# A prompt and sample step of a hybrid decoder: the sample's state updates in four row tiles, C against both halves of the states in one bank

## Chip, cores and metric

One core of a Trainium2 chip runs the whole step. The metric is the device time of one execution in microseconds; lower is better. The kernel before was timed in three runs.

## What is computed

One layer of a decoder trunk on a prompt of 16 + 256 tokens and on 8 samples of 4 tokens each: a SwiGLU block, a token mixer and a second SwiGLU block, each behind an RMSNorm. The mixer has a gated short convolution and a state-space branch. All matrices are float32; the kernel multiplies in a split of each operand into a high and a low part. The part that matters here is the state-space branch for the samples, in which the carried state of each sample (32 heads x 64 x 128) is read by C and brought up to date:

```python
xdt = x * dtc[..., None]
decay = jnp.exp(acs[:, :, -1:] - acs)
states = jnp.einsum('bcsgn,bcsgr,bcsgrp->bcgrpn', bc, decay, xdt)
chunk_decay = jnp.exp(acs[:, :, -1])
def step(h, inp):
    s, d = inp
    return h * d[..., None, None] + s, h
y_off = jnp.einsum('bcqgn,bcgrpn,bcqgr->bcqgrp', cc, h_prev, jnp.exp(acs))
```

For a sample, `states` sums over 4 tokens only, and there is one chunk. The new state of all 8 samples is an output of 8 MB, as is the old one an input.

## The kernel before

**The main stream.** `program` lists all products with weights as tiles of 128 x 128, in order: ffn1, the input projection (ga, dt, x, ac, ah, ab), ya, z, gb, yb, wo, ffn2. `drive` (L231) walks that list. Each tile is three matmuls (L255 to L257): high weight by high input, high by low, low by high, into a PSUM bank of the pool `psm` (4 banks, tag "m"). Weights come by DMA on SP, 8 tiles at a time, and are split three such units ahead: ACT copies the high part (L183), DVE subtracts (L184).

**The side work.** Two generators do the state-space scan beside the main stream: `Scan.prompt` for the prompt and `Scan.sample` for the samples, and before them `Scan.setup`. `drive` counts up `wanted["due"]` by a rate per main tile and calls `side_step` for each whole one: it takes the generators in turn and lets one run to its next `yield`. From ac to z (384 main tiles) the rate is RATE2. What is left when gb comes is emitted by `flush_side`. The side's PSUM banks are those of the pool `pss` (4 banks, tag "s").

**Order.** The code's order is not yet the order on an engine: the tile framework schedules each engine's instructions by priority in program order and by a simulated readiness, so that a side matmul that is not ready lets main matmuls pass. On the chip each engine then runs its list in order.

**The sample's part.** The 8 samples are two halves q of four samples j. For each group g of 8 heads the 4 states of a half lie in `ht`, [128 state rows, 4 samples, 512], loaded by `load` and stored by `store` on SP (L1051, L1104), with three buffers.
- `tokens(g)` (L1068) turns the group's x into rows of tokens by four transposes (L1078), multiplies by dt (L1082) and by the decay (L1060), and splits it into `xst`; then the same for the prompt's last 16 tokens into `xl`.
- For each half (L1113 on): `bm` is B masked for each of the four samples (L1125). C times the four states (L1131) goes to four strips of 32 columns of one bank. ACT copies it (L1133), four transposes (L1138) turn it, and DVE multiplies it into `yo` (L1141).
- For each sample: DVE decays the state (L1150), one matmul of `bm[:, j]` and `xst` over all 128 rows makes the update (L1152), DVE adds it (L1153). Each update has a bank of its own.
- At the end of a group DVE finishes the sample's y and calls `ready`; once the z tiles, two prompt `outputs` and the sample of a group are through, its norm is made, and after gb `scaled_splits` (L299, L300, L293) makes the operands of yb.

**The prompt's part.** For each half group `hg`: `tokens`, `weights`, `states` (L983 to L991), `outputs` (L1003 to L1021), each of one or a few steps.

**The set-up.** `setup` makes dt, the cumulated decays and the rows of B in the x stage, with small matmuls over 16, 32 or 128 rows (L781 to L807).

## Time and profile before

| | us |
|---|---|
| median of three runs | 881.52 (880.02 to 881.68) |
| the profiled execution | 881.86 |
| its span, from the first to the last instruction | 880.0 |
| PE busy | 868.8 (99%) |
| DVE busy | 621.3 (71%) |
| ACT busy | 496.2 (56%) |

The span is what the profile sees of one execution; the time has a little before and after it. Busy time is time in which an engine has at least one instruction under way. Matmuls overlap each other in a row of them, so that the sum of their durations is more than the time they take; the distance between two starts is what one costs. The scan runs beside the stages ac to z, from about 350 to 557 us; gb follows to 583 us, then yb.

### The profile page before, as it was taken

How to read it: one execution, taken by the hardware profiler on the slowest of the kernel's cores; microseconds unless marked ns; L12 is line 12 of the kernel's file. 1: busy time of each engine (PE TensorE's matmuls, PEld its weight loads, DVE VectorE, ACT ScalarE, POOL GpSimd, SP SyncE). 2: the span in 40 equal slices, each digit the busy share in tenths (PEclk: the TensorE clock that was granted, in tenths of full speed). 3: DMA queues.
4: the chain of work that ended last, by engine and by line, in shares of the span. 5: the costliest groups of instructions: out<-in, count | busy, mean ns of one | idle time of the engine just before them, and what ended most of it. 6: DMA issues, size and time to landing. Idle time of an engine off the chain costs nothing.

```text
span 880.0 us, 16239 instructions
## 1 busy us (share of the span) xinstructions
PE 868.8 (99%) x6448; PEld 849.8 (97%) x6448; DVE 621.3 (71%) x996; ACT 496.2 (56%) x899; POOL 53.4 (6%) x86
## 2 busy tenths in 40 slices
PE   9999999999999999999999999999999999999996
PEld 7999999999999999999999899999999999999996
DVE  6756666554677798799988999886676666665443
ACT  8543434343667787966655687774465444444442
POOL 0000000000012233001000211100000000000000
PEclk9999999999999999999999999999999999999999
DMA  8554545454644545865666655755555555555541
GB/s 299 190 155 157 165 147 167 146 166 150 201 166 146 153 153 171 314 211 202 231 223 225 242 198 174 257 183 169 167 168 166 164 165 166 163 164 168 169 139 54
DMA packets 45851, 158.69 MB, mean 180 GB/s; under 512 B 7168, under 2 KB 9504, under 8 KB 43472
## 3 DMA queue, kind: packets, MB, share of 16 engines
q1 hardware_dynamic: 45344, 157.21, 54.6%
q8 instruction: 50, 0.82, 0.4%
q10 hardware_dynamic: 432, 0.46, 0.2%
q14 instruction: 25, 0.20, 0.1%
HBM read 145.34 MB, written 12.31 MB: 179 GB/s over the span
## 4 chain that ended last, share of the span: by engine, by line
PE 97%; DVE 1%; ACT 1%; DMA 1%; SPq 0%; issue 0%; DVEq 0%
PE ps_d L257 6%; PE ps_d L256 5%; PE ps_d L255 5%; PE ps_u L257 5%; PE ps_g L255 5%; PE ps_u L256 5%; PE ps_u L255 5%; PE ps_g L257 5%; PE ps_g L256 5%; PE ps_x L255 3%; PE ps_x L256 3%; PE ps_x L257 3%; PE ps_z L255 2%; PE ps_z L257 2%; PE ps_yb L257 2%; PE ps_yb L255 2%
## 5 line engine op out<-in xcount | busy, mean ns | idle before, releaser
L184 DVE TENSOR_TENSOR wlo<-wraw,whi 128x1024 fp32r<-128x1024 f32 (+2 forms) x250 | 300.6, 1204 | 188.8 <-ACT whi L183 188.1
L183 ACT ACTIVATE whi<-wraw 128x1024 fp32r<-128x1024 f32 (+2 forms) x250 | 259.6, 1041 | 296.8 <-issue 182.8
L257 PE MATMUL ps_d<-hh,wlo 128*128 128x304 f32 (+1 forms) x352 | 105.6, 300 | 0.0
L255 PE MATMUL ps_d<-hh,whi 128*128 128x304 f32 (+1 forms) x352 | 105.0, 299 | 0.0
L256 PE MATMUL ps_d<-hl,whi 128*128 128x304 f32 (+1 forms) x352 | 104.7, 298 | 0.0
L256 PEld LDWEIGHTS ps_d<-hl,whi 128*128 128x128 f32 x352 | 66.7, 189 | 0.0
L257 PEld LDWEIGHTS ps_d<-hh,wlo 128*128 128x128 f32 x352 | 66.2, 188 | 0.0
L255 PEld LDWEIGHTS ps_d<-hh,whi 128*128 128x128 f32 x352 | 66.1, 188 | 0.0
L255 PE MATMUL ps_x<-unh,whi 128*128 128x304 f32 x192 | 58.8, 309 | 0.7 <-ACT dtraw L735 0.7
L256 PE MATMUL ps_x<-unl,whi 128*128 128x304 f32 x192 | 58.8, 307 | 0.0
L257 PE MATMUL ps_x<-unh,wlo 128*128 128x304 f32 x192 | 58.6, 306 | 0.0
L255 PE MATMUL ps_g<-n1h,whi 128*128 128x304 f32 x176 | 54.1, 308 | 0.7 <-ACT whi L183 0.7
L256 PE MATMUL ps_u<-n1l,whi 128*128 128x304 f32 x176 | 53.6, 304 | 0.0
L255 PE MATMUL ps_u<-n1h,whi 128*128 128x304 f32 x176 | 53.5, 304 | 0.0
L256 PE MATMUL ps_g<-n1l,whi 128*128 128x304 f32 x176 | 53.4, 304 | 0.0
L257 PE MATMUL ps_g<-n1h,wlo 128*128 128x304 f32 x176 | 53.1, 303 | 0.0
L257 PE MATMUL ps_u<-n1h,wlo 128*128 128x304 f32 x176 | 52.9, 302 | 0.0
L257 PE MATMUL ps_g<-n2h,wlo 128*128 128x288 f32 x176 | 52.3, 297 | 0.0
L255 PE MATMUL ps_u<-n2h,whi 128*128 128x288 f32 x176 | 52.2, 297 | 0.0
L257 PE MATMUL ps_u<-n2h,wlo 128*128 128x288 f32 x176 | 52.1, 296 | 0.0
L255 PE MATMUL ps_g<-n2h,whi 128*128 128x288 f32 x176 | 51.9, 295 | 0.0
L256 PE MATMUL ps_u<-n2l,whi 128*128 128x288 f32 x176 | 51.4, 292 | 0.0
(342 smaller groups left out, 2435.6 us busy)
## 6 DMA issues: line engine op xcount, KB each, us to landing
wraw<-wst SPq DMA_DIRECT2D x241, 512.0 KB, 3.5
h<-h SPq DMA_DIRECT2D x8, 1024.0 KB, 5.0
o_hs<-h SPq DMA_DIRECT2D x8, 1024.0 KB, 4.3
acb<-cumd SPq DMA_DIRECT2D x8, 512.0 KB, 4.3
wraw<-wst SPq DMA_DIRECT2D x7, 256.0 KB, 6.4
hd<-h SPq DMA_DIRECT2D x1, 1216.0 KB, 6.6
h<-hd SPq DMA_DIRECT2D x1, 1216.0 KB, 8.3
o_hp<-hf SPq DMA_DIRECT2D x8, 128.0 KB, 2.8
```

The lines of the kernel that those rows point to most:

```text
L183: act.activation(hi[:, a:b], r[:, a:b], AF.Copy)
L184: dve.tensor_tensor(out=lo[:, a:b], in0=r[:, a:b], in1=hi[:, a:b].bitcast(F32), op=ALU.subtract)
L255: te.matmul(o, lhsT=wh, rhs=xh, start=first, stop=False)
L256: te.matmul(o, lhsT=wh, rhs=xl, start=False, stop=False)
L257: te.matmul(o, lhsT=wl, rhs=xh, start=False, stop=last)
```

## The change

- C times the states is done once for each group: both halves accumulate in one bank, the second half's rows beside the first's, by a C operand that is zero elsewhere (`cc`). There are four evictions by ACT and 16 transposes of its result.
- The rows of tokens are laid out anew (`rows`, `sample_rows`): each strip of 32 rows has the tokens of two samples, one of each half, four times over (the parts of the split). `bm` masks by half only, so there are two masks per group. The update of sample j uses rows 32j to 32j + 31 alone.
- The four updates of a half go out as one group, j from 3 to 0, in four banks: three of `pss` and one of `psm`. Each is kept in program order behind the matmul traced before it, and the next main matmul behind them (`pin`).
- All decays of a half are done before. The step before the updates sets `hold`, and the prompt's generator idles at its yields until the updates are out.
- The prompt's last 16 tokens share one layout with the samples' 32 rows (`mixed`, `mixed_rows`); the small matmuls of the set-up use 48 rows, and column masks `kd` are added up there.
- `store` is called one step before the updates of the next half. RATE2 goes from 0.33 to 0.36.

```diff
-RATE2 = 0.33
+RATE2 = 0.36
...
-                te.matmul(o, lhsT=wh, rhs=xh, start=first, stop=False)
+                ins = te.matmul(o, lhsT=wh, rhs=xh, start=first, stop=False)
+                if clock.pop("pin", False):
+                    tc.keep_in_program_order(ins)
...
+    ssd.pin = lambda: clock.update(pin=True)
...
+        self.mixed(reps[:, 0:1], raw.unsqueeze(1))
+        self.rows(xp, reps[:, 1:2], raw[:, S0:T].unsqueeze(1))
...
-        dl = da[0:NL, 2]
+        dx = da[0:NX, 2]
         te.matmul(pv[:, 0], lhsT=K[:, C_GT:C_GT + P], rhs=da[:, 0], start=True, stop=True)
         te.matmul(pv[:, 1], lhsT=K[:, C_GT:C_GT + P], rhs=da[:, 1], start=True, stop=False)
-        te.matmul(pv[:, 1], lhsT=K[0:NL, C_ONE:C_ONE + P], rhs=dl, start=False, stop=True)
-        te.matmul(pv[:, 2], lhsT=gtl.rearrange("p k t -> p (k t)"), rhs=dl, start=True, stop=True)
-        te.matmul(pv[:, 3], lhsT=K[0:32, C_GTS:C_GTS + P], rhs=da[0:32, 3], start=True, stop=True)
+        te.matmul(pv[:, 1], lhsT=one, rhs=dx, start=False, stop=True)
+        te.matmul(pv[:, 2], lhsT=gtl, rhs=dx, start=True, stop=True)
+        te.matmul(pv[:, 3], lhsT=gtr, rhs=dx, start=True, stop=True)
         te.matmul(pv[:, 4], lhsT=K[:, C_ONE:C_ONE + P], rhs=da[:, 1], start=True, stop=False)
-        te.matmul(pv[:, 4], lhsT=K[0:NL, C_ONE:C_ONE + P], rhs=dl, start=False, stop=True)
+        te.matmul(pv[:, 4], lhsT=one, rhs=dx, start=False, stop=True)
...
+        kd = self.kd = self.t("kd", [P, 6])
+        for i, bs in enumerate(((4, 5, 6, 7), (2, 3, 6, 7), (0, 2, 4, 6), (1, 3, 5, 7))):
+            dve.tensor_tensor(out=kd[:, i:i + 1], in0=K[:, C_BM + bs[0]:C_BM + bs[0] + 1],
+                              in1=K[:, C_BM + bs[1]:C_BM + bs[1] + 1], op=ALU.add)
+            for b in bs[2:]:
+                dve.tensor_tensor(out=kd[:, i:i + 1], in0=kd[:, i:i + 1], in1=K[:, C_BM + b:C_BM + b + 1], op=ALU.add)
+        dve.tensor_scalar(out=kd[:, 4:6], in0=kd[:, 0:2], scalar1=2.0, scalar2=-1.0, op0=ALU.mult, op1=ALU.add)
+        dve.tensor_tensor(out=kd[:, 5:6], in0=kd[:, 4:5], in1=kd[:, 5:6], op=ALU.mult)
+
...
+    def mixed(self, out, x):
+        act, n = self.nc.scalar, out.shape[1]
+        k = P // NL - 2
+        act.activation(out[:, :, 0:NB * NT], x[:, :, S0:T], AF.Copy)
+        for j in range(n):
+            act.activation(out[:, j, NB * NT:].rearrange("p (k t) -> p k t", t=NL),
+                           x[:, j, TL:S0].unsqueeze(1).to_broadcast([P, k, NL]), AF.Copy)
+    def rows(self, pl, out, x):
+        act, (p, n, _) = self.nc.scalar, out.shape
         self.n += 1
-        r = pl.tile([P, 4, P // n, n], F32, name=f"four{self.n}", tag="tmp", bufs=2)
-        src = self.xs[:, c0:c0 + 4, a:a + n].unsqueeze(2).to_broadcast([P, 4, P // n, n])
-        for j in range(4):
-            self.nc.scalar.activation(r[:, j], src[:, j], AF.Copy)
-        return r.rearrange("p j k t -> p j (k t)")
+        t = pl.tile([p, n, 4, 2, NT], F32, name=f"rows{self.n}", tag="rows", bufs=1)
+        for q in range(2):
+            act.activation(t[:, :, :, q], x[:, :, 16 * q:16 * q + 16].rearrange("p n (i t) -> p n i t", t=NT), AF.Copy)
+        for j in range(n):
+            act.activation(out[:, j].rearrange("p (i c w) -> p i c w", c=4, w=2 * NT),
+                           t[:, j].rearrange("p i q t -> p i (q t)").unsqueeze(2).to_broadcast([p, 4, 4, 2 * NT]),
+                           AF.Copy)
+    def sample_rows(self, pl, c0):
+        self.n += 1
+        r = pl.tile([P, 4, P], F32, name=f"srows{self.n}", tag="tmp", bufs=2)
+        self.rows(pl, r, self.xs[:, c0:c0 + 4, S0:T])
+        return r
...
+        for _ in steps():
+            yield
+            while self.hold:
+                yield
...
-        def splits(name, pv, dtr, bufs):
-            xr = self.t("xrs", [P, 8, HD], bufs=2, tag="tmp")
-            dve.tensor_tensor(out=xr, in0=pv, op=ALU.mult, in1=dtr.unsqueeze(2).to_broadcast([P, 8, HD]))
-            xf = xr.rearrange("p h d -> p (h d)")
-            o = self.t(name, [P, 512], bufs=bufs, dt=F32R)
-            act.activation(o, xf, AF.Copy)
-            dve.tensor_tensor(out=o[64:P], in0=xf[64:P], in1=o[64:P].bitcast(F32), op=ALU.subtract)
-            return o
         def tokens(g):
             hs = slice(8 * g, 8 * g + 8)
-            xt[g] = self.t("xdts", [NX, 8, HD])
-            for o, i in ((xst, 3), (self.xl, 2)):
-                if i == 2:
-                    rep[g] = self.four(self.sp, 4 * g, True)
-                    yield
+            def turned(src):
                 p = self.ps()
-                src = rep.pop(g)
                 for j in range(4):
                     te.transpose(p[:, j * P:(j + 1) * P], src[:, j], ident)
-                del src
-                pv = p.rearrange("p (h d) -> p h d", h=8)
-                a = slice(0, NS) if i == 3 else slice(NS, NX)
-                dve.tensor_tensor(out=xt[g][a], in0=pv[a], op=ALU.mult,
-                                  in1=self.dt[a, i, hs].unsqueeze(2).to_broadcast([a.stop - a.start, 8, HD]))
-                if i == 2:
-                    while self.xl:
-                        yield
-                o[g] = splits("xst" if i == 3 else "xl", pv, self.dtr[:, i, hs], i - 1)
+                return p.rearrange("p (h d) -> p h d", h=8)
+            def decayed(pv, i, a):
+                xr = self.t("xrs", [P, 8, HD], bufs=2, tag="tmp")
+                dve.tensor_tensor(out=xr[a], in0=pv[a], op=ALU.mult,
+                                  in1=self.dtr[a, i, hs].unsqueeze(2).to_broadcast([a.stop - a.start, 8, HD]))
+                return xr.rearrange("p h d -> p (h d)")
+            xf = decayed(turned(rep.pop(g)), 3, slice(0, P))
+            o = xst[g] = self.t("xst", [P, 512], bufs=2, dt=F32R)
+            act.activation(o, xf, AF.Copy)
+            dve.scalar_tensor_tensor(out=o, in0=xf, scalar=self.kd[:, 0:1], in1=o.bitcast(F32), op0=ALU.mult,
+                                     op1=ALU.subtract)
+            del xf
+            m = self.mixed_rows(self.sp, 4 * g)
+            yield
+            pv = turned(m)
+            del m
+            xt[g] = self.t("xdts", [NX, 8, HD])
+            dve.tensor_tensor(out=xt[g], in0=pv[0:NX], op=ALU.mult,
+                              in1=self.dt[0:NX, 2, hs].unsqueeze(2).to_broadcast([NX, 8, HD]))
+            while self.xl:
                 yield
+            xf = decayed(pv, 2, slice(64, P))
+            o = self.xl[g] = xlt
+            act.activation(o[64:P], xf[64:P], AF.Copy)
+            dve.tensor_tensor(out=o[96:P], in0=xf[96:P], in1=o[96:P].bitcast(F32), op=ALU.subtract)
+            yield
...
-        for u in range(2 * G):
-            g, q = divmod(u, 2)
+        for g in range(G):
             gs = slice(4 * g, 4 * g + 4)
-            ht = hts[u]
-            if q == 0:
-                cc = self.t("cc", [P, 2 * NS], bufs=2)
-                act.activation(cc.rearrange("p (k t) -> p k t", k=2),
-                               xs[:, XC + G + g, S0:T].unsqueeze(1).to_broadcast([P, 2, NS]), AF.Copy)
-            bm = self.t("bm", [P, 4, P], dt=F32R)
-            for j in range(4):
-                b = C_BM + 4 * q + j
-                act.activation(bm[:, j], self.bs[:, g].bitcast(F32), AF.Copy, scale=K[:, b:b + 1])
+            act.activation(cc.rearrange("p (q w) -> p q w", q=2)[:, :, 0:P].rearrange("p q (j r) -> p q j r", j=4)
+                           [:, :, :, 0:NT],
+                           xs[:, XC + G + g, S0:T].rearrange("p (q j t) -> p q j t", q=2, j=4), AF.Copy)
+            bm = self.t("bm", [P, 2, P], dt=F32R)
+            for q in range(2):
+                act.activation(bm[:, q], self.bs[:, g].bitcast(F32), AF.Copy, scale=self.kd[:, 2 + q:3 + q])
             p = self.ps()
-            for j in range(4):
-                a = 4 * NT * q + NT * j
-                te.matmul(p[32 * j:32 * j + 32], lhsT=cc[:, a:a + NS], rhs=ht[:, j], start=True, stop=True)
+            for q in range(2):
+                for j in range(4):
+                    te.matmul(p[32 * j:32 * j + 32], lhsT=cc[:, P * q + 32 * j:P * q + 32 * j + 32],
+                              rhs=hts[2 * g + q][:, j], start=q == 0, stop=q == 1)
             yr = self.t("yr", [P, 4, P], tag="tmp", bufs=2)
             act.activation(yr, p.rearrange("p (c n) -> p c n", c=4), AF.Copy)
             yield
             p = self.ps()
             for c in range(4):
                 te.transpose(p[:, c * P:(c + 1) * P], yr[:, c], ident)
-            y, ec = (t[:, gs, 4 * NT * q:4 * NT * (q + 1)].rearrange("p c (b t) -> p c b t", b=4)
-                     for t in (yo, self.ec))
-            dve.tensor_tensor(out=y, in0=p.rearrange("p (c b n) -> p c b n", c=4, b=4)[:, :, :, 0:NT], in1=ec,
-                              op=ALU.mult)
+            del yr
+            for q in range(2):
+                y, ec = (t[:, gs, 4 * NT * q:4 * NT * (q + 1)].rearrange("p c (b t) -> p c b t", b=4)
+                         for t in (yo, self.ec))
+                dve.tensor_tensor(out=y, in0=p.rearrange("p (c b n) -> p c b n", c=4, b=4)[:, :, :, NT * q:NT * q + NT],
+                                  in1=ec, op=ALU.mult)
+            if g + 1 < G:
+                rep[g + 1] = self.sample_rows(self.sp, 4 * g + 4)
             yield
-            if q == 0 and g + 1 < G:
-                rep[g + 1] = self.four(self.sp, 4 * g + 4)
-            for j in range(4):
-                o = ht[:, j]
-                oh = o.rearrange("p (h d) -> p h d", h=8)
-                dec = self.dec[:, 8 * g:8 * g + 8, 4 * q + j].unsqueeze(2).to_broadcast([P, 8, HD])
-                dve.tensor_tensor(out=oh, in0=oh, in1=dec, op=ALU.mult)
-                p = self.ps()
-                te.matmul(p, lhsT=bm[:, j], rhs=xst[g], start=True, stop=True)
-                dve.tensor_tensor(out=o, in0=p, in1=o, op=ALU.add)
+            for q in range(2):
+                ht = hts[2 * g + q]
+                for j in range(4):
+                    oh = ht[:, j].rearrange("p (h d) -> p h d", h=8)
+                    dec = self.dec[:, 8 * g:8 * g + 8, 4 * q + j].unsqueeze(2).to_broadcast([P, 8, HD])
+                    dve.tensor_tensor(out=oh, in0=oh, in1=dec, op=ALU.mult)
+                    if j == 1:
+                        yield
+                self.hold = True
                 yield
-                if q == 1 and j == 1 and g + 1 < G:
-                    yield from tokens(g + 1)
-                if q == 1 and j == 3 and g + 1 < G:
-                    diagonal(g + 1)
-                    yield
-            late.append(u)
-            if q == 1:
-                y = xs[:, gs, S0:T]
-                ds = V[:, V_DS + 4 * g:V_DS + 4 * g + 4].unsqueeze(2).to_broadcast([P, 4, NS])
-                dve.tensor_tensor(out=yo[:, gs], in0=yo[:, gs], in1=self.yd[g][:, :, 0:NS], op=ALU.add)
-                dve.tensor_tensor(out=y, in0=y, in1=ds, op=ALU.mult)
-                dve.tensor_tensor(out=y, in0=y, in1=yo[:, gs], op=ALU.add)
-                self.ready(g)
+                store()
+                yield
+                ps = [(self.pss if j else self.psm).tile([P, 512], F32, name=f"up{g}_{q}_{j}",
+                                                        tag="s" if j else "m") for j in range(4)]
+                for j in range(3, -1, -1):
+                    a = slice(32 * j, 32 * j + 32)
+                    ins = te.matmul(ps[j], lhsT=bm[a, q], rhs=xst[g][a], start=True, stop=True)
+                    self.tc.keep_in_program_order(ins)
+                self.pin()
+                self.hold = False
+                for j in range(3, -1, -1):
+                    dve.tensor_tensor(out=ht[:, j], in0=ps[j], in1=ht[:, j], op=ALU.add)
+                del ps
+                yield
+                yield
+                late.append(2 * g + q)
+                if q == 0:
+                    y = xs[:, gs, S0:T]
+                    ds = V[:, V_DS + 4 * g:V_DS + 4 * g + 4].unsqueeze(2).to_broadcast([P, 4, NS])
+                    dve.tensor_tensor(out=yo[:, gs], in0=yo[:, gs], in1=self.yd[g][:, :, 0:NS], op=ALU.add)
+                    dve.tensor_tensor(out=y, in0=y, in1=ds, op=ALU.mult)
+                    dve.tensor_tensor(out=y, in0=y, in1=yo[:, gs], op=ALU.add)
+                    self.ready(g)
+            if g + 1 < G:
+                yield from tokens(g + 1)
+                diagonal(g + 1)
+                yield
```

## Rows read from the trace of the kernel before

**Rows 1.** The page's part 4: the chain that ended last, by engine.
```profile
PE 97%; DVE 1%; ACT 1%; DMA 1%; SPq 0%; issue 0%; DVEq 0%
```

**Rows 2.** Busy us of each engine by stage (x; ac to ya; z; gb).
```profile
core 0: us, PE busy (x) PEld busy (x) DVE busy (x) ACT busy (x) POOL busy (x), PEclk, DMA share, GB/s
252.00:350.00 98.00, 97.34 (x704) 96.55 (x703) 78.22 (x126) 76.94 (x173) 27.00 (x44) 0.98 0.52 158
350.00:482.00 132.00, 131.78 (x1036) 124.31 (x1035) 117.50 (x217) 86.28 (x193) 8.91 (x15) 1.00 0.67 234
482.00:560.00 78.00, 78.00 (x607) 71.20 (x607) 74.02 (x134) 59.63 (x124) 12.01 (x9) 1.00 0.59 205
560.00:590.00 30.00, 30.00 (x227) 29.89 (x226) 26.02 (x46) 24.24 (x42) 3.56 (x3) 1.00 0.68 231
```

**Rows 3.** Groups of instructions, PE: busy, mean ns, idle before, releaser.
```profile
L257 PE MATMUL ps_ya<-ya,wlo 128*128 128x288 f32 x64 | 18.8, 300 | 0.2 <-DVE wlo L184 0.2
```

**Rows 4.** Timeline, PE: start, duration, one update and its successor.
```profile
498.46 0.39 PE L1152 MATMUL sps<-xst,bm 128*128 128x512 f32 x1
498.69 0.29 PE L257 MATMUL ps_z<-unh,wlo 128*128 128x288 f32 x1
```

**Rows 5.** Groups of instructions, PE: updates, C, and its transposes, with counts.
```profile
L1152 PE MATMUL sps<-xst,bm 128*128 128x512 f32 x32 | 13.8, 448 | 0.0
...
L1131 PE MATMUL sps<-h,cc 128*32 128x512 f32 x64 | 8.5, 605 | 0.0
...
L1138 PE MATMUL sps<-K,yr 128*128 128x128 f32 x32 | 4.8, 274 | 0.0
```

**Rows 6.** Timeline, PE: one C group between main matmuls.
```profile
549.54 0.29 PE L257 MATMUL ps_z<-unh,wlo 128*128 128x288 f32 x1
549.76 1.06 PE L1131 MATMUL sps<-h,cc 128*32 128x512 f32 x8
550.76 0.40 PE L255 MATMUL ps_z<-unh,whi 128*128 128x288 f32 x1
551.00 0.30 PE L256 MATMUL ps_z<-unl,whi 128*128 128x288 f32 x1
551.13 0.30 PE L257 MATMUL ps_z<-unh,wlo 128*128 128x288 f32 x1
```

**Rows 7.** The chain in order of time: start, us, what.
```profile
418.63 0.43 PE sps L984 x2
```

**Rows 8.** Timeline, PE: small matmuls of the set-up.
```profile
279.24 0.38 PE L784 MATMUL sps<-dta,gtl 16*128 16x32 f32 x2
279.46 0.38 PE L785 MATMUL sps<-dta,K 32*128 32x32 f32 x2
```

**Rows 9.** Timeline, PE: four transposes between main matmuls.
```profile
497.49 0.29 PE L256 MATMUL ps_z<-unl,whi 128*128 128x288 f32 x1
497.62 0.60 PE L943 MATMUL sps<-K,xs 128*128 128x128 f32 x4
497.98 0.38 PE L257 MATMUL ps_z<-unh,wlo 128*128 128x288 f32 x1
498.20 0.29 PE L255 MATMUL ps_z<-unh,whi 128*128 128x288 f32 x1
```

**Rows 10.** Groups of instructions, DVE: the adds of the updates.
```profile
L1153 DVE TENSOR_TENSOR h<-sps,h 128x512 f32<-128x512 f32 x32 | 21.5, 680 | 1.1 <-PE sps L1152 1.1
```

**Rows 11.** Waits of SP's queue: us in total, times, longest.
```profile
SPq L1104 <- DVE h L1153: 8.2, 4, 3.4
```

**Rows 12.** Timeline, PE and DVE: an update and its add.
```profile
378.26 0.48 PE L1152 MATMUL sps<-xst,bm 128*128 128x512 f32 x1
...
382.16 0.67 DVE L1153 TENSOR_TENSOR h<-sps,h 128x512 f32<-128x512 f32 x1
```

**Rows 13.** yb: its first start (min/median/max ns, first to last), the last splits.
```profile
L255 PE MATMUL ps_yb<-ynh,whi x128: 290/297/299, 583.8 to 634.2; 128*128 128x288 f32 x128
...
590.11 0.93 DVE L293 SCALAR_TENSOR_TENSOR ynl<-g_t,V,ynh 128x288 fp32r<-128x288 f32 x2
```

More of the change, by code (lines that the diff above doesn't have):

```diff
@@ L1108, in sample @@
             load(u)
-        rep[0] = self.four(self.sp, 0)
+        xlt = self.t("xl", [P, 512], dt=F32R)
+        act.activation(xlt[0:64], K[0:64, 0:512], AF.Copy, scale=0.0)
+        cc = self.t("cc", [P, 2 * (P + NT)])
+        pool.memset(cc, 0.0)
+        rep[0] = self.sample_rows(self.sp, 0)
         yield
```

113 lines of the change are left out of this document (59 added, 54 removed).

## The prediction

> **What bounds the kernel now.** I read the page's chain first: 97% of the span is on the matmul engine (PE) [rows 1]. Then the busy time by stage: from 350 to 590 us, where the change works, PE is busy in all but 0.22 us, while DVE has 117.5 of 132 us in the first stretch and 74.0 of 78 in the second [rows 2]. The reader is to see two things: PE has no idle time to win, and DVE is a close second. The only wait of PE named there is 0.2 us for a weight split on DVE [rows 3]. So the edit is worth the PE time that it removes, less what PE newly waits.
>
> "Busy" does not price one matmul, since the records overlap. The price is the distance from one start to the next. An ordinary matmul of the main stream takes 0.13 us (551.00 to 551.13 in [rows 6]). One state update between two of them takes 498.69 - 498.46 = 0.23 us [rows 4].
>
> **The updates, moved into row tiles.** There are 32 [rows 5], in 8 groups of four: 4 x 0.23 = 0.92 us a group, 7.4 in all. After the change a group is four matmuls that use 32 rows each and could run side by side. The trace has no row-tiled group. Its nearest relative is the C group, four column tiles of 32 columns:
> - From 549.54 to 551.00 is 1.46 us; the two ordinary matmuls at its edges are 0.27 of it, so the group costs 1.19 [rows 6]. Two 256-column fp32 records take 0.43 us [rows 7], so one 512-column fp32 matmul alone would take 0.86. Four took 1.19 together, not 3.4: tiles do run side by side, and going into the tile shape and out again costs 1.19 - 0.86 = 0.33 us (0.09 before the first start, 0.11 where the next full matmul loads its weights openly, the rest inside).
> - An update loads 128 weight columns per tile where C loads 32, so I add one open load, 0.11 us, the amount by which the full matmul after the group is late (551.00 - 550.76 = 0.24 against 0.13).
>
> So a group is 0.23 + 0.33 + 0.11 = 0.67 us, and 8 groups save 8 x (0.92 - 0.67) = **2.0 us**. Bounds: with that load hidden 0.56 (2.9 saved); with the four loads one after another but the streams overlapped 0.67 + 3 x 0.11 = 1.00 (0.6 lost); with no overlap at all 4 x (0.23 + 0.11) + 0.33 = 1.69 (6.2 lost). For the last speak the small matmuls of 16 and 32 rows, which follow each other at 0.11 us a record (279.46 - 279.24 for two) [rows 8]; but all of them use the same rows, where nothing could overlap. The C group is nearer in length and shape, so I take 0.67.
>
> The Trainium skill ("TensorE: Matmul & The Clock Gate", section "Measured speedup vs the span model") gives 3.07 times for four row tiles of 512 columns. By that, as an estimate, the group's streams take 4 x 0.23 / 3.07 = 0.30 us in place of my 0.34, and the sum would be 0.3 us better. No run here shows it yet. Against the change speaks "TensorEngine Tiling (Array Packing)", section "Key Properties": a change of tiling mode drains the engine. The trace agrees, with 0.33 us per C group.
>
> **C times both halves in one bank.** The same 32 matmuls, 64 records [rows 5], but four groups in place of eight. Streaming is the same; four switches go: 4 x 0.33 = **1.3 us**. The transposes of its result halve, 32 to 16 [rows 5]. Four transposes cost 498.20 - 497.49 - 0.27 = 0.44 us [rows 9], so 16 are 16 x 0.11 = **1.75 us**. On ACT four of eight evictions go. What it adds: C now needs two states loaded. The load of the second is issued with the store step of the group before, some 30 tiles of main work ahead (a tile is three matmuls, 0.4 us).
>
> **The rest, at nothing.** The block masks are 8 ACT copies in place of 32, against a few more ACT copies for the replicated rows; ACT has 86.3 of 132 us [rows 2], and that room is the cover. Per group of heads one of two DVE products of 512 elements a partition goes, about the 0.68 us of a 512-element add [rows 10], 2.7 us in all. The small set-up matmuls change rows from 16 and 32 to 48 and switch about as often. The new columns `kd` are 14 one-column DVE operations in the x stage, where DVE has 78.2 of 98 us [rows 2]; without that cover they would cost under their own length, a few us at most, and I take nothing. State stores and loads stay on SP, in a step of their own some 10 tiles or more behind the adds. Before, SP stood 8.2 us there for the adds, with weight loads queued behind [rows 11]; that wait should shrink, and costs nothing now.
>
> **What is added as a wait.** The four updates and the next main matmul are chained on PE. They need three of the four side banks and one of the four main banks at once, freed by DVE and ACT. Whatever main work stands behind the pin on PE waits with it, and then its evictions and the weight splits. A side result can lie long before DVE comes to it: the update at 378.26 was added at 382.16, 3.9 us later [rows 12]. The cover is the pause: I count about 11 tiles, 11 x 0.4 = 4.4 us, between the step that raises `hold` and the updates, in which the prompt issues nothing. That is just over the 3.9. So I allow half of the seen 0.2 us wait per group, 8 x 0.1 = **0.8 us** (ends: 0, and the case below).
>
> **Pace.** The side work has 384 main tiles (ac to z). At 0.33 that is 126.7 steps, at 0.36 it is 138.2. Counting the yields, before needs 66 for the sample and 56 for the prompt, with a few waiting ones; after needs 62 + 56 + 16 idle. Both fit, and both end with z. But the last step is now the prompt's last `outputs`, where it was the sample's last update. Next late would be group 3's norm and its splits for yb: the last splits start at 590.11 where yb starts at 583.8 [rows 13], and scaled rows 14 and 15 alone are that late while two output tiles offer 2 x 15 x 0.4 = 12 us of other matmuls. So some 5 us of slack cover it.
>
> **Sum.** 2.0 + 1.3 + 1.75 - 0.8 = 4.25 us less. The profiled execution took 881.86 us (span 880.0), 0.34 over the median of 881.52: 877.6 on its scale, **877.3 us** on the median's.
>
> **Rivals.**
> 1. *The loads go one after another*: -0.6 in place of +2.0, so 881.5 - (3.05 - 0.6 - 0.8) = 879.9 us.
> 2. *DVE becomes the bound.* The 32 adds of 0.68 us [rows 10] stay, and four come in one burst. In z DVE has 74.0 of 78 us [rows 2]; the share of the gain that falls there, 78/210 of 5.05 = 1.9 us, would need 97% of DVE. If z gives all of it back and the denser stretch before it as much again, 881 us. For it: the one PE wait was for DVE [rows 3]. Against: DVE loses 2.7 us too. The Trainium skill ("TensorEngine Tiling (Array Packing)", section "PSUM Bottleneck") says the same: tiling speeds the matmuls, and their eviction may become the limit.
> 3. *The row tiles run one after another*: the change doesn't do what it says; 6.2 lost against 3.05 won and 0.8 of waits, 885.5 us, slower. Against: the C group's overlap.
> 4. *The pinned group waits for its banks*, the slower case by a wait. It turns at 5.05 / 8 = 0.63 us per group, and is slower by over 0.2% from (5.05 + 1.8) / 8 = 0.85. With a third of the 3.9 us, 1.3 a group, it is 881.5 - 5.05 + 10.4 = 886.9 us. For it: the lag of 3.9 us. Against: the pause is longer than it.
>
> **How the numbers follow.** A measurement of this kernel tells about 0.2% (1.8 us) from no change. Forecast 877.3 (874.5 to 879.5): 0.51. Rival 1: 0.12. Rival 2: 0.19. Rival 3: 0.07. Rival 4: 0.11. The low end is the 2.9 bound without waits, 875.6, less a run's spread of 1; the high end 882.5 takes in rivals 1 and 2, and leaves out 3 and 4. Faster (under 879.7): the forecast, half of rival 1, a third of 2: 0.63. Slower (over 883.3): 3 and 4 less a little: 0.17. Same: 0.20.
>
> **What would show it.** Right: in the timeline four update records start within some 0.03 us of each other, the next full matmul about 0.6 us later; half the transposes; PE still busy without gaps before them. Wrong: starts 0.1 us or more apart (rival 1), 0.3 apart (3), idle PE ahead of the first update with a DVE or ACT release (4), or PE waits in z for the splits (2).

## The result: 0.5% slower, and where it shows in the profile

| | before | after |
|---|---|---|
| median of four runs, us | 881.6 | 886.23 |
| range | 880.02 to 882.27 | 885.23 to 886.75 |
| span of the profiled execution, us | 880.0 | 884.7 |

The ratio is 1.0054 (95% interval 1.0036 to 1.0071). The forecast was 877.3 us: the change costs 4.6 us where 4.25 were to be gained. The time lies outside the range (the prediction names two high ends, 879.5 and 882.5 us) and near the fourth rival's 886.9 us, which had a chance of 0.11.

First the chain that ended last, by engine (the page's part 4), and the busy times by stage, with the columns of [rows 2]:

```profile
PE 91%; ACT 4%; DVE 3%; issue 1%; DMA 1%; SPq 0%; DVEq 0%; ACTq 0%
```

```profile
350.00:482.00 132.00, 126.12 (x986) 115.60 (x985) 116.59 (x217) 82.82 (x191) 7.53 (x16) 0.97 0.66 230
482.00:560.00 78.00, 78.00 (x611) 73.17 (x610) 67.47 (x117) 53.30 (x105) 11.06 (x9) 1.00 0.63 217
...
380.00:390.00 10.00, 6.03 (x28) 4.99 (x28) 8.45 (x21) 0.44 (x1) 0.00 (x0) 0.66 0.18 72
```

Against [rows 1] PE has lost 6% of the chain to ACT, DVE and issue; against [rows 2] it is now idle for 5.9 us between 350 and 482 us, where it had 0.22. From 482 to 560 us it stays full. So the loss is in one place, and the last row finds it: from 380 to 390 us PE is busy for 6 of 10 us, and its granted clock is 0.66 in the mean. DVE has 67.5 us of work from 482 to 560 us in place of 74.0, but z begins 8.7 us later now, and this stretch begins in ya. By z's own bounds (before, then after) it is 71.2 of 75.2 us before and 60.5 of 68.5 after:

```profile
482.21:557.41 75.20, 75.20 (x587) 68.48 (x586) 71.22 (x128) 57.14 (x121) 12.01 (x9) 1.00 0.60 209
490.92:559.42 68.50, 68.50 (x542) 63.78 (x540) 60.53 (x106) 50.33 (x101) 11.06 (x9) 1.00 0.60 206
```

The groups of instructions on PE show who is waited for (columns as in [rows 3] and [rows 5]):

```profile
L1183 PE MATMUL sps<-h,cc 128*32 128x512 f32 x64 | 7.7, 598 | 0.0
L1220 PE MATMUL up<-xst,bm 32*128 32x512 f32 x32 | 5.6, 521 | 4.5 <-DVE yo L1196 4.1 <-DVE xr L987 0.4
L1191 PE MATMUL sps<-K,yr 128*128 128x128 f32 x16 | 2.5, 275 | 0.9 <-ACT yr L1186 0.9
```

32 updates (L1220), 64 records of C (L1183) and 16 transposes (L1191) are there as foreseen, and the updates have 4.5 us of idle time ahead of them, which ended with two DVE operations. The timeline of PE shows that it is one group, the first (start, duration, engine and line, what, count, and in brackets the idle time before):

```profile
372.57 0.30 PE L259 MATMUL ps_ac<-unh,wlo 128*128 128x290 f32 x1
373.40 0.67 PE L1146 MATMUL sps<-ms,xdts 48*64 48x48 f32 x16 [0.54 <-DVE xdts L1131]
374.00 1.92 PE L1183 MATMUL sps<-h,cc 128*32 128x512 f32 x16
376.78 0.66 PE L1191 MATMUL sps<-K,yr 128*128 128x128 f32 x4 [0.85 <-ACT yr L1186]
...
378.67 0.49 PE L1220 MATMUL up<-xst,bm 32*128 32x512 f32 x1
379.09 0.38 PE L1025 MATMUL sps<-xl,bl 128*128 128x256 f32 x1
383.53 0.76 PE L1220 MATMUL up<-xst,bm 32*128 32x512 f32 x1 [4.05 <-DVE yo L1196]
384.73 0.79 PE L1220 MATMUL up<-xst,bm 32*128 32x512 f32 x2 [0.44 <-DVE xr L987]
385.45 0.61 PE L255 MATMUL ps_ah<-unh,whi 128*128 128x290 f32 x1
385.86 0.44 PE L258 MATMUL ps_ah<-unl,whi 128*128 128x290 f32 x1
```

From 372.57 to 385.45 us no main matmul runs. PE has come to the first group and finds the side's whole chain still under way in front of it: diagonal, C, its eviction, the transposes, then the updates one by one as banks come free. The run of side matmuls holds the main stream for 385.86 - 372.57 - 2 x 0.13 = 13.0 us; the same matmuls without a wait cost 5.1 (the run e5 below: 2.65 and 2.49 by the same measure). So **7.9 us** go there. Behind it the main matmuls stand 0.24 us apart instead of 0.13 (386.10 follows 385.86, and so on to 388.27 us), the lower of the clock's two levels: 11 of them take **1.1 us** more. (The expectations below put 1.3 for it, with the step from 385.45 to 385.86, which is in the 13.0 already.) The granted clock, the third number from the right, fell inside the idle stretch, so that the last updates ran at the lower level too, 0.76 us long in place of 0.5, and that is in the 7.9:

```profile
376.00:381.00 5.00, 2.70 (x14) 1.94 (x14) 4.91 (x9) 2.77 (x10) 0.97 (x1) 1.00 0.65 214
382.00:384.00 2.00, 0.47 (x1) 0.28 (x1) 2.00 (x6) 0.00 (x0) 0.00 (x0) 0.50 0.00 0
```

What DVE did meanwhile, its timeline:

```profile
377.66 2.50 DVE L1206 TENSOR_TENSOR h<-h,dec 128x512 f32<-128x512 f32 x4
380.19 0.42 DVE L544 TENSOR_TENSOR yat<-ps_ab,cva 128x256 f32<-128x256 f32 x1
380.53 0.18 DVE L545 TENSOR_TENSOR yat<-ps_ab,cva 128x32 f32<-128x32 f32 x1
380.63 2.49 DVE L1206 TENSOR_TENSOR h<-h,dec 128x512 f32<-128x512 f32 x4
383.04 0.34 DVE L1196 TENSOR_TENSOR yo<-sps,ec 128x64 f32<-128x64 f32 x2
383.30 0.68 DVE L987 TENSOR_TENSOR xd<-sps,dtt 128x512 f32<-128x512 f32 x1
383.90 0.68 DVE L987 TENSOR_TENSOR xr<-sps,dtr 128x512 f32<-128x512 f32 x1
```

Eight decays of 0.62 us, four of each half, run ahead of `yo` (L1196) and `xr` (L987). These two free the banks that the updates need. The second half's decays aren't due before the first half's updates are out; the scheduler had them ready and put them first.

The other seven groups stand without a wait, the third one at 430.45 us for instance:

```profile
430.23 0.29 PE L259 MATMUL ps_ab<-unh,wlo 128*128 128x288 f32 x1
430.45 0.50 PE L1220 MATMUL up<-xst,bm 32*128 32x512 f32 x4
430.88 0.40 PE L255 MATMUL ps_ab<-unh,whi 128*128 128x288 f32 x1
431.11 0.30 PE L258 MATMUL ps_ab<-unl,whi 128*128 128x288 f32 x1
```

The four starts are 3 to 4 ns apart, and a group costs 431.11 - 430.23 - 2 x 0.13 = 0.62 us, 0.62 to 0.64 over the seven.

### The profile page after: what moved, and what is told of

It reads as the page before. It is cut to its first block, busy times and chain, and to the rows that moved or that the text cites. A ratio compares the mean times of both kernels' runs of the same rounds, so it can differ in the third digit from the quotient of the medians.

```text
span 884.7 us, 16212 instructions
## 1 busy us (share of the span) xinstructions
PE 866.3 (98%) x6428; PEld 845.8 (96%) x6428; DVE 620.2 (70%) x1002; ACT 491.1 (56%) x894; POOL 62.3 (7%) x87
## 4 chain that ended last, share of the span: by engine, by line
PE 91%; ACT 4%; DVE 3%; issue 1%; DMA 1%; SPq 0%; DVEq 0%; ACTq 0%
PE ps_d L259 5%; PE ps_d L258 5%; PE ps_d L255 5%; PE ps_u L259 5%; PE ps_g L255 5%; PE ps_u L258 5%; PE ps_u L255 5%; PE ps_g L259 5%; PE ps_g L258 5%; PE ps_x L255 3%; PE ps_x L258 3%; PE ps_x L259 3%; PE ps_yb L259 2%; PE ps_yb L255 2%; PE ps_yb L258 2%; PE ps_z L255 2%
```

## The experiments

Each was timed against the kernel before in the same rounds (medians of before 881.0 to 881.5). Theory A: the side's chain lags, and the group's ties hold the main stream until it has come. Theory B: what the group waits for is DVE's order, the block of eight decays. Theory C: the pins cost something at every group. Theory D: DVE is at its bound and gives the gain back.

| | median, us | ratio to before (95%) |
|---|---|---|
| e1 next main matmul not pinned | 886.74 | 1.0055 to 1.0082 |
| e6 banks of the side alone, pins kept | 888.20 | 1.0069 to 1.0095 |
| e5 banks of the side alone, main not pinned | 884.14 | 1.0030 to 1.0055 |
| e2 no pins at all | 884.58 | 1.0026 to 1.0062 |
| e3 first group free | 882.67 | 1.0004 to 1.0037 |
| e7 first group's decays in order | 882.81 | 1.0011 to 1.0037 |
| e4 start 30 tiles later | 880.25 | 0.9977 to 0.9997 |
| e8 the two together | 881.16 | 0.9987 to 1.0012 |
| e14 start 50 later | 879.50 | 0.9971 to 0.9992 |
| **e9 start 60 later** | **876.90** | **0.9944 to 0.9972** |
| e14 start 70 later | 881.59 | 0.9998 to 1.0018 |
| e12 start 90 later | 880.64 | 0.9985 to 1.0010 |
| e10 the kernel before, start 60 later | 886.49 | 1.0046 to 1.0071 |
| e11 e9 with C for each half | 879.99 | 0.9980 to 0.9997 |
| e13 longer pause at the first group | 893.79 | 1.0131 to 1.0157 |
| **e16 start 30, all decays in order** | **877.66** | **0.9947 to 0.9975** |
| e17 start 60, all decays in order | 878.38 | 0.9963 to 0.9981 |
| e18 start 70, all decays in order | 882.74 | 1.0011 to 1.0032 |

### What holds the main stream at the group

```diff
-                self.pin()
```

> The one line that pins the next main matmul behind a group of updates is left out; the four updates stay chained among themselves. In the changed kernel one side run of the matmul engine, at 373.4 us, costs 13.0 us where its matmuls are worth 5.4, and the clock falls behind it. Theory A: the first pinned group is reached by the main stream before the scan's late chain has come that far, and the main stream is held there twice over, by the pin and by the bank that the group takes from the main pool, in whose order the next output tiles stand behind it. By A the time stays where it is, within 1 us of the changed kernel's 886.2, with the same idle time ahead of the first group. Theory P: the pin alone holds the main stream; then about 877.5 us and no idle time.

Measured 886.74 us, the same idle time (4.1 us ahead of the first group, for `yo`). The pin of the next main matmul isn't needed for the wait.

```diff
-                ps = [(self.pss if j else self.psm).tile([P, 512], F32, name=f"up{g}_{q}_{j}",
-                                                        tag="s" if j else "m") for j in range(4)]
+                ps = [self.pss.tile([P, 512], F32, name=f"up{g}_{q}_{j}", tag="s") for j in range(4)]
```

> The changed kernel with all four banks of a group from the side's pool and the pins kept. Of the two ties to the main stream the first run left the bank alone (886.7 us), this one leaves the pin alone, and the run without either had no idle time but came apart (884.1 us). Theory A: the pin alone holds the main stream as well, 886 us (885 to 887.5), with the same idle time ahead of the first group. If the main pool's bank were needed for it: no idle time there and 877 to 884 us.

888.2 us, a little above the range: again 4.0 us for `yo`, and 1.2 more elsewhere (a weight split ahead of ya). So either tie holds the main stream alone, as long as the four updates are chained. With both edits neither tie is left:

> All four banks of a group of updates come from the side's pool and the next main matmul is not pinned: neither tie to the main stream is left, and main matmuls can pass a late group. The four updates stay chained. Theory A (the main stream is held at the first group, by the pin and by the main pool's bank): the idle time goes, 877.5 us (876.5 to 879); in the trace main matmuls stand between the first group's transposes and its updates. Theory C (row tiles and their mode switches cost more than the parts they replace, at every group): 884 to 887 us, since the eight groups are still there. Theory D (DVE gives the gain back late, in z and gb): 881 to 883 us.

884.14 us, a miss by 6.6, though PE has no idle time left from 370 to 560 us. The reason stands in its timeline:

```profile
477.57 0.29 PE L259 MATMUL ps_ya<-ya,wlo 128*128 128x288 f32 x1
477.79 0.49 PE L1219 MATMUL up<-xst,bm 32*128 32x512 f32 x1
478.21 0.40 PE L255 MATMUL ps_ya<-ya,whi 128*128 128x288 f32 x1
478.45 0.30 PE L258 MATMUL ps_ya<-ya,whi 128*128 128x288 f32 x1
```

One tile costs 478.45 - 477.57 - 0.27 = 0.61 us, and four that stay together cost 0.63 here too. The way into the tile shape and out of it is the price, the other three tiles are nearly free. Of the 32 updates only two groups stayed whole, the rest came apart into some 21 more runs: 23 x 0.62 = 14.3 us in place of 5.0. The 9.3 us eat the wait that went: from the first start of ac to that of yb this trace takes 239.3 us, that of the changed kernel 239.7. The next run tells the same without any pin:

```diff
-                    self.tc.keep_in_program_order(ins)
-                self.pin()
```

> No update and no main matmul is pinned; the banks stay as in the change (three of the side's pool, one of the main pool). The updates then stand in 22 runs on the matmul engine, most of them single. Theory A with the price of 0.62 us a run, however many tiles are in it: 14 more runs than eight cost 8.7 us, and the idle time of 9.0 us goes, so 886.2 - 9.0 + 8.7 = 885.9 us (884 to 887.5), with PE never idle. If a single row tile cost only what an ordinary update costs between main matmuls before (0.23 us): 22 x 0.23 = 5.1 us for all of them, about what eight groups cost, and 877.5 us.

884.58 us, within the range of theory A; the single updates cost 0.61 to 0.63 each. Without pins the groups come apart, with them the main stream waits; here the pins cost a little more than they save (886.2 us against 884.6). Freeing the first group alone:

```diff
-                    self.tc.keep_in_program_order(ins)
-                self.pin()
+                    if g or q:
+                        self.tc.keep_in_program_order(ins)
+                if g or q:
+                    self.pin()
```

> Only the first of the eight groups is neither chained nor followed by a pinned main matmul; the other seven are as in the change. Its four updates then come apart, with main matmuls between them: eleven runs of updates on the matmul engine in place of eight. With all banks from the side's pool, single row tiles cost 0.62 us each where a whole group costs 0.63. Theory A: the idle time of the first group and the low clock go (7.7 + 1.3 us), and three more runs of 0.62 us come: 886.2 - 9.0 + 1.9 = 879.1 us (878 to 880.5). Theory C (the pins of the other groups cost too): 883 us or more.

882.67 us where 879.1 was expected. The wait didn't go, it moved: the second group, still pinned, waited 1.4 us, and the transposes of the next group's tokens 1.6 us for ACT.

### Is it the lag, or DVE's order?

```diff
-RATE2 = 0.36
+RATE2 = 0.391
...
+    wanted["due"] = -30 * RATE2
```

> The scan's steps begin 30 main tiles (about 12 us) later, at a rate of 0.391 in place of 0.36, so that they end where they ended. Pins, banks and groups stay. Theory A (the main stream reaches the first pinned group before the scan's late chain has come that far): with 12 us more of main work ahead of it the idle time of about 7.7 us and the 1.3 us of low clock behind it go: 877.5 us (876.5 to 879). Theory B (what holds the first group is DVE's own order, in which the half's y product stands behind eight decays, and not the start): about half of the idle time stays, 881 to 883 us. Theory C (the pins cost a little at each of the eight groups): no change, 885 to 887 us.

880.25 us: most of the wait went, not all. PE's timeline at the first group:

```profile
386.64 0.30 PE L259 MATMUL ps_ah<-unh,wlo 128*128 128x290 f32 x1
386.87 1.08 PE L1221 MATMUL up<-xst,bm 32*128 32x512 f32 x2
389.02 0.50 PE L1221 MATMUL up<-xst,bm 32*128 32x512 f32 x2 [1.06 <-DVE xr L988]
389.45 0.40 PE L255 MATMUL ps_ah<-unh,whi 128*128 128x290 f32 x1
389.69 0.29 PE L258 MATMUL ps_ah<-unl,whi 128*128 128x290 f32 x1
```

The group costs 389.69 - 386.64 - 0.27 = 2.78 us, 2.15 too many, and the low clock returns behind it, from 390.25 to 393.4 us. Again the eight decays stood on DVE ahead of `xr`; they ended at 385.5 us, and 2.7 us of other work came between, the main stream's weight split among it.

```diff
-                    dve.tensor_tensor(out=oh, in0=oh, in1=dec, op=ALU.mult)
+                    ins = dve.tensor_tensor(out=oh, in0=oh, in1=dec, op=ALU.mult)
+                    if not g:
+                        self.tc.keep_in_program_order(ins)
```

> For the first group of heads the eight decays on DVE are kept in program order, so that the y product and the two products for the prompt's rows, which free the banks that the first updates wait for, are no longer behind all of them. Pins and banks stay. Theory A: the chain is late anyway and only the part of the idle time that these decays made goes, 4.05 + 0.44 us of the 7.7 and perhaps some of the low clock: 881 us (880 to 883). Theory B (DVE's order is the whole cause): 877.5 us. If the four decays only trade places with other work that the updates need: no change, 886 us.

882.81 us, at the upper end of theory A's range: the 4.05 us for `yo` are gone, 2.3 for `xr` have come in their place.

> Both cures together: the scan begins 30 main tiles later (rate 0.391) and the first group's decays on DVE are kept in program order. With the later start alone the first group still waited 2.15 us (a cost of 2.78 where the other groups cost 0.63), half of it for a product on DVE that stood behind eight decays in one block, and some 13 main matmuls behind it ran at the low clock at 0.24 in place of 0.13 us, 1.4 us. Theory A (a late chain at the first group, and nothing else): both go, 880.25 - 2.15 - 1.4 = 876.7 us (876 to 878), all eight groups at 0.62 to 0.64 us. If DVE, 25 of 25 us busy from 370 to 395, only moves its backlog to the next group (theory D): 879 to 881 us, with a wait at the second or third group.

Both edits together: 881.16 us, a miss for theory A and close to theory D's 879 to 881. The first group cost 1.13 us and the low clock behind it was gone. The wait stood at the third group now, 2.0 and 0.9 us by the starts of its updates, with low clock behind it; there the decays weren't ordered (DVE, then PE):

```profile
424.60 4.90 DVE L1207 TENSOR_TENSOR h<-h,dec 128x512 f32<-128x512 f32 x8 [0.66 <-PE sps L1184]
427.94 0.50 PE L1223 MATMUL up<-xst,bm 32*128 32x512 f32 x1
429.93 1.66 PE L1223 MATMUL up<-xst,bm 32*128 32x512 f32 x3 [1.50 <-DVE t L1053]
```

The starts in between and beyond, by the two lines of e4's diff with other numbers:

```diff
-RATE2 = 0.36
+RATE2 = 0.427
...
+    wanted["due"] = -60 * RATE2
```

> The scan begins 60 main tiles (about 25 us) later than in the changed kernel, at a rate of 0.427, with the same last step; nothing else. Theory A: the tail of the x stage is worked off on ACT and DVE before the first group, so the wait at it goes, and with it the low clock: 877 us (876 to 878.5). Theory D (DVE is near its bound over the whole scan, 117.5 of 132 us before; a denser scan only moves the wait): waits of DVE at later groups or splits, 879 to 882 us.

> The scan begins 90 main tiles later than in the changed kernel, at a rate of 0.47. After 0, 30 and 60 tiles the medians were 886.2, 880.25 and 876.9 us. Theory A (the wait was the scan's lag at a pinned group, and at 60 tiles none is left): no further gain, 877 us (876 to 878.5), all groups at 0.62 to 0.64 us. Theory D (a denser scan loads DVE until splits or a group wait again): 879 to 882 us.

> The scan begins 50 main tiles later at a rate of 0.414. If a later start removes the lag step by step: between the 880.25 of 30 tiles and the 876.9 of 60, 877 to 878.5 us, with no wait or one under 1 us at the groups. If 60 tiles was one lucky alignment of the groups with the DVE's work: 879 to 882 us, with a wait of 1 us or more at some group.

> The scan begins 70 main tiles later at a rate of 0.440. If the optimum is broad: 876.5 to 878.5 us. If 60 tiles was one lucky alignment: 879 to 882 us, with a wait of 1 us or more at some group, as at the third one with 90 tiles.

60 tiles gave 876.9 us, the best of all and what theory A expected there; 50, 70 and 90 gave 879.5, 881.6 and 880.6, each with a wait at the third group. So 60 is an alignment and not an optimum of the lag. The third group with 70 tiles (DVE, then PE):

```profile
433.69 4.91 DVE L1207 TENSOR_TENSOR h<-h,dec 128x512 f32<-128x512 f32 x8 [1.59 <-PE sps L1184]
438.51 0.46 DVE L1053 TENSOR_TENSOR t<-sps,eb 128x288 f32<-128x288 f32 x1
...
440.44 0.87 DVE L1059 SCALAR_TENSOR_TENSOR xs<-xs,V,sps 128x256 f32<-128x256 f32 x2
```

```profile
437.43 0.50 PE L1221 MATMUL up<-xst,bm 32*128 32x512 f32 x1
439.02 0.50 PE L1221 MATMUL up<-xst,bm 32*128 32x512 f32 x1 [1.09 <-DVE t L1053]
441.46 0.79 PE L1221 MATMUL up<-xst,bm 32*128 32x512 f32 x2 [1.94 <-DVE xs L1059]
```

and with 60 tiles:

```profile
429.49 4.90 DVE L1207 TENSOR_TENSOR h<-h,dec 128x512 f32<-128x512 f32 x8
...
436.24 0.86 DVE L1059 SCALAR_TENSOR_TENSOR xs<-xs,V,sps 128x256 f32<-128x256 f32 x2
```

```profile
437.17 0.56 PE L1221 MATMUL up<-xst,bm 32*128 32x512 f32 x4
```

Both times a block of eight decays, 4.9 us, stands ahead of `t` and `xs`, which free the banks. With 70 tiles PE was at the group in the middle of the block; with 60 `xs` ended at 437.1, and the group began at 437.17 us. The runs with all decays in order (e7's diff, without its `if`) take the block apart at every group:

> The scan begins 30 main tiles later (rate 0.391) and all decays on DVE, of every group, are kept in program order: the second half's four come behind the first half's adds, and not in one block of eight ahead of both. With the first group's alone in order it took 881.2 us, with a wait of some 2.9 us at the third group and low clock behind it (1.4 us). If the block of eight decays is what a group waits for (theory B): that goes too, 877 us (876 to 878.5). If the side's chain is late as such and the wait moves on to another group (theory A): 880 to 882 us.

> As the last one, with the scan begun 60 tiles later (rate 0.427), where the time without ordered decays was 876.9 us and no group waited. Both theories: 876.5 us (875.5 to 878), as there is no wait to take away; under theory A a changed order of DVE's work may bring a wait back, 879 to 881 us.

> As the last one, with 70 tiles (rate 0.440), where without ordered decays it took 881.6 us: the third group waited 4.0 us (1.6 and 2.4) behind a block of eight decays, and some low clock followed. Theory B (the block): 876.5 us (875.5 to 878), the same as with 60 tiles. Theory A (the alignment of the start): 880 us or more, with the wait still at the third group.

The first speaks for theory B: 877.66 us against 881.16 with the first group alone in order. The groups' idle time is 0.2 us by their line, some 1.2 by their starts (0.64 at the first, 0.54 at the third). With 70 tiles the expectation hits at the group and misses in the total. The third group's wait fell from 1.09 + 1.94 us to

```profile
439.29 0.50 PE L1222 MATMUL up<-xst,bm 32*128 32x512 f32 x2 [0.35 <-DVE xs L1059]
```

but ya then waited for its weight splits on ACT (the waits of PE: total, times, longest):

```profile
PE ps_ya L255 <- ACT whi L183: 2.6, 2, 2.2
```

and 882.74 us is no better than 881.59. With 60 tiles it misses at both: a wait of 0.8 us came to the third group, 878.38 us. So the block of decays makes most of the wait at three groups, by the starts of their updates: at the first with the start 30 tiles later (2.15 us in e4, 0.5 in e8), at the third with that start (2.9 in e8, 0.5 in e16), at the third with 70 tiles (4.0 us, 0.9 in e18). It isn't the whole cause. In the changed kernel it is 3.1 of the 7.9 us (the first run of side matmuls costs 9.9 us in e7 in place of 13.0, the low clock within it included), and with 60 tiles the third group waits without a block (e17) where it didn't with one (e9). What sets the other waits, and with them the best start, is left open.

The last test of the lag is a longer pause:

```diff
-RATE2 = 0.36
+RATE2 = 0.381
...
-                yield
+                for _ in range(9 if g + q == 0 else 1):
+                    yield
```

> The changed kernel with the pause before the first group of updates longer by eight steps (about 21 main tiles, 8.4 us, at a rate of 0.381 so that the last step stays where it was); start, pins and banks as in the change. If the wait at the first group was the lag of the side's chain, larger than the pause that was counted as its cover: 8.4 us more cover take away the 7.7 us of idle time and the 1.3 us of low clock, 877.5 us (876.5 to 879). If the chain behind the first group then stands at the next one: 879 to 882 us, with a wait at the second or third group. If the cause lies in the early start, whatever the pause: 884 us or more.

893.79 us. Here the expectation miscounted: the pause idles the prompt's generator too, so eight steps take sixteen of the count, and the rate allowed for eight. The last steps spilled over the end of z, where PE waited 4.3 us for one operation of POOL alone, and z took 84.7 us by the first starts of z and gb (68.5 in the changed kernel). What the run does show is the part before that: with the longer pause the first seven groups cost 0.63 to 0.64 us each, the very first included. A pause that is long enough does cover the lag.

### Controls: the late start alone, and the C part

On the kernel before:

```diff
-RATE2 = 0.33
+RATE2 = 0.391
...
+    wanted["due"] = -60 * RATE2
```

> A control: the kernel before, without any part of the change, with its scan begun 60 main tiles later (rate 0.391 in place of 0.33, the same last step). If the later start helps only because it takes away the wait of a pinned group (theory A), nothing is to be had here, since main matmuls pass a late update in that kernel: within 1.5 us of before. If a later start is a gain of its own, 2 to 5 us less than before, and the 876.9 of the changed kernel with the later start wouldn't speak for the change.

886.49 us, outside both expectations: the late start costs the kernel before 5.5 us. Its scan isn't done when gb comes. There 41 matmuls that aren't the main stream's stand in gb where 4 stood, PE waits for an eviction by ACT that comes late (3.1 us), and the stretch from gb to yb takes 35.9 us in place of 26.4. So a late start is no gain for this kernel, but what it would be worth without that spill isn't shown. That the gain of e9 is the change's is read from the terms in its trace (groups at 0.62 to 0.69 us, C for both halves at 2.05, 16 transposes at 0.11) and from one of them undone. On e9, C for each half:

```diff
-            p = self.ps()
+            yrs = []
             for q in range(2):
+                p = self.ps()
                 for j in range(4):
                     te.matmul(p[32 * j:32 * j + 32], lhsT=cc[:, P * q + 32 * j:P * q + 32 * j + 32],
-                              rhs=hts[2 * g + q][:, j], start=q == 0, stop=q == 1)
+                              rhs=hts[2 * g + q][:, j], start=True, stop=True)
...
```

> One part undone, on the changed kernel with the scan begun 60 tiles later (876.9 us): C times the states goes again once for each half, in a bank of its own, with its own eviction on ACT, four transposes and a product on DVE. By the terms of the sum this brings back four mode switches at 0.33 us and 16 transposes at 0.11 us: 3.1 us more, 880 us (879 to 881). In the trace each half's C group costs about 1.2 us and its transposes 0.44. If the C part were worth nothing, 877 us.

879.99 us, 3.1 more, just as expected, and yet not by the terms expected. The groups of instructions on PE:

```profile
L1185 PE MATMUL sps<-h,cc 128*32 128x512 f32 x64 | 7.7, 598 | 0.0
L1197 PE MATMUL sps<-K,yr 128*128 128x128 f32 x32 | 4.7, 274 | 0.0
```

By the distances of starts the side's matmuls cost 2.9 us more. The 16 transposes are back, 0.44 us per four, 1.75 us. But the two halves' C stood side by side on PE, and the 16 records cost 2.05 us together, no more than in one bank: none of the 1.3 us of switches came back. The rest is small: 0.45 us of wait at the third group, 0.7 spread out. Where the C groups stood apart, in the kernel before, one cost 1.19 [rows 6], two 2.38.

## Why the prediction was wrong, step by step

- **The updates, 0.67 us a group: right.** Measured 0.62 to 0.64; 8 x (0.92 - 0.63) = 2.3 us saved, 2.0 forecast. The third rival (one after another) is out: the four starts lie within some 10 ns. The first (loads one after another) is out too. The bound that took that load as hidden, 0.56, was nearly as close as the value taken.
- **C in one bank, 1.3 + 1.75 us: right in size.** Both halves cost 2.05 us where they cost 2 x 1.19. The transposes halved at 0.11 each. By e11 the 1.3 comes from the halves standing together, for which one bank isn't needed.
- **DVE as the bound (second rival): not seen in z, where it was put.** There DVE fell from 71.2 of 75.2 us to 60.5 of 68.5, and PE stayed full.
- **The wait, 0.8 us: this step failed.** It was put down as 0.1 us at each of eight groups, covered by a pause. It was 7.9 us at one group, 1.1 of low clock behind it and 0.4 for a weight split in gb, 9.4 in all. With it the sum is 881.5 - (2.3 + 1.3 + 1.75) + 9.4 = 885.55 us; 886.23 was measured. The two traces say nearly the same: from the first start of ac to that of yb they take 235.9 us before and 239.7 after, 3.8 more, where 9.4 - 5.35 is 4.05. So 5.35 us of gain were there, in the place of the forecast's 5.05.

What was wrong in that step, as it was put:
1. "The cover is the pause": 4.4 us against a lag of 3.9 [rows 12]. The pause was counted in the program, about 11 tiles, which are 33 main matmuls. On PE it wasn't there: between the first group's transposes (376.78) and its updates (378.67) no main matmul stands, while the third group has 33 and waits for nothing. All kernels that tie the groups to the main stream show this: ten have a group with none between, and it waited 0.5 to 6.9 us by the starts of its updates; of the groups with 24 or more only two waited over 0.1 us (the third of e1, the second of e3). The lag, too, was read from one update and its add, with DVE free of anything that the change adds. The change itself puts eight decays, 5.0 us, ahead of what frees the banks, and that alone is more than the pause. The text had the decays in its list of the change and no term for their order on DVE. With a longer pause (e13), 72 main matmuls by the trace, the first group doesn't wait; with a later start and the decays in order (e16) it waits 0.6 us.
2. The mean of a long stretch hid the place. "DVE has 117.5 of 132 us" [rows 2] leaves room; from 370 to 395 us, where the first groups stand, there was none in the kernel before already (the row below). There it cost nothing, as main matmuls passed the late update. The change takes just that freedom away.
3. A wait was spread evenly over eight groups, "half of the seen 0.2 us wait per group". It came whole at one, and the clock fell in it, for which the sum had no term.

The busy time of the kernel before in that stretch, 24.88 of 25 us on DVE:

```profile
370.00:395.00 25.00, 25.00 (x200) 22.20 (x199) 24.88 (x45) 17.79 (x40) 1.56 (x4) 1.00 0.60 193
```

The fourth rival had the mechanism and the releaser (DVE). That its 886.9 us lies so near is luck: its price, 1.3 us at each of eight groups, was the same thought of an even wait. Its chance of 0.11 leaned on the comparison of 4.4 with 3.9, a margin of 0.5 us read from one instance.

Six versions beat both kernels (e4, e14 with 50 tiles, e11, e17, e9, e16). The two best, e9 (876.9 us) and e16 (877.66 us), reach the forecast's time by the forecast's terms, once the wait is nearly gone.

## What to carry to other kernels

A matmul that may not be passed turns every lag of the engine that frees its banks into idle time of TensorE: before pinning, read how busy that engine is in the very stretch, and what the change puts on it ahead of the freeing operations, and not a mean over the stage. A pause counted in the program covers a lag only if its matmuls stand between on the engine: look for them in the timeline. When row tiles are worth their switch only as a group, they need to be tied together; then take the other engine's work that isn't due yet out of the way, and look for the wait again at every later group. A total that comes out as expected doesn't prove its terms: look in the trace whether each of them is there.

## What the runs showed of the hardware

- A single row tile of 512 columns between full matmuls costs 0.61 us, a group of four 0.63. One update as a full-row matmul cost 0.23 [rows 4]. So going into the shape and out again costs about 0.4 us, once for each run of tiles, and the further tiles are nearly free. The Trainium skill ("TensorEngine Tiling (Array Packing)", section "Key Properties") says that a change of mode drains the engine; these runs agree with it, with those 0.4 us over the ordinary update. The Trainium skill ("TensorE: Matmul & The Clock Gate", section "Measured speedup vs the span model") puts the span of a pack at one matmul and some 4 ns for each further tile; the starts here, 3 to 4 ns apart, agree with that.
- PE's clock fell to the lower of its two levels (1.2 of 2.4 GHz) in or behind an idle stretch. In the changed kernel the granted clock was 1.00 from 376 to 381 us, where PE was busy for 2.70 of 5 us, and 0.50 from 382 to 384; 11 main matmuls behind the group took 1.1 us more at it. With the start 30 tiles later (e4) it was 1.00 from 385 to 390 us, where PE was busy for 3.82 of 5, and 0.50 from 390.25 to 393.4, for 13 main matmuls and 1.4 us. It doesn't fall behind every wait: with the start 50 tiles later PE waited 1.9 us at the third group, was busy for 3.06 us from 431 to 436, and the granted clock stayed at 1.00. A wait at a group can thus be dearer than its length.
